# A decoder layer on one core: two of its norms read features-first inputs

## The chip, the cores and the metric

The kernel runs on one core of a Trainium2 chip. The core has a tensor engine (PE, with its weight loads listed as PEld), a vector engine (DVE), a scalar engine (ACT), GpSimd (POOL) and SyncE (SP), which here only issues transfers. Each engine has its own queue of instructions and takes them in order; semaphores hold an instruction until its inputs are there. DMA engines move data between main memory and the on-chip memory of 128 partitions; transfers are issued from the queues of SP, ACT and POOL. Matmuls write to eight PSUM banks of 128 x 512 fp32.

The metric is the device time of one execution in microseconds (us), and the median over several runs.

## What is computed

One layer of a decoder for 256 tokens of 2048 features, in fp32. Cut to what matters here:

```python
def rms_norm(x, g):
    y = x * rsqrt(mean(x * x, axis=-1) + 1e-6)
    return y * g

def swiglu(h, w_gate, w_up, w_down):
    return (silu(h @ w_gate) * (h @ w_up)) @ w_down

x = x + 0.5 * swiglu(rms_norm(x, ffn1_norm), ffn1_w_gate, ffn1_w_up, ffn1_w_down)
x = gated_parallel_mixer(x, mix_norm, w_in, ...)   # attention beside RWKV-7, then w_out
h, mn = rms_norm(x, cross_norm), rms_norm(mem, mem_norm)
x = x + attend(h @ w_cross_q, mn @ w_cross_kv) @ w_cross_o
x = x + 0.5 * swiglu(rms_norm(x, ffn2_norm), ffn2_w_gate, ffn2_w_up, ffn2_w_down)
return rms_norm(x, final_norm)
```

`x` and `mem` are both 256 x 2048. The feed-forward width is 5632. Five norms feed products; the change concerns the two that read inputs of the kernel, that of `x` in front of the first feed-forward and that of `mem`.

## The kernel before

**Products.** PE contracts over partitions, so the activations of a product must lie features first: 16 chunks of 128 features, each a tile of 128 features x 256 tokens. To keep fp32 accuracy each operand is split in a high half (rounded to the matmul's type) and a low half, the difference; `times` (line 426) issues three matmuls per chunk: high by high (L429), high by low (L430), low by high (L431). A `multiply` does two chunks for one half of the tokens, that is six matmuls; an *item* is two chunks of one block of 512 weight columns, so it has two multiplies, twelve matmuls. A product over 2048 features has eight items.

**Weights.** SP loads raw weights into buffers (`load`, tag raw2 with three buffers, two items each, in the feed-forward), ACT casts them to the high half (L341), DVE subtracts to the low half (L342). `next_item` loads ahead and splits up to two items ahead of the one in use; high and low halves have three buffers each.

**The order of work.** `Interleave` holds side jobs as generators in groups (const, feat, attn, ew, chain, norm, mem, in this order). Every multiply is followed by one `tick`, in which each group steps its first jobs once. `product` ticks until the chunks of an item are there (`x.done`), then issues the item. Issue order on the engines follows this, except that an instruction may be put ahead of an earlier one that has to wait; `tc.issue_after` forbids this against one given instruction.

**The norms.** A `Norm` scales by the gain while the data are moved and applies the factor 1/rms later, at the product's result, since it is one number per token. `block` handles 512 features: for two chunks at a time `feat` (L626) makes four PE transposes of 128 x 128 into a PSUM bank, ACT writes the high half times the gain (L653), DVE the low half (L654). Then two ACT squares with a sum along the row (L662) give the sums of squares per token. After the fourth block `rstd` adds the four sums (L672), scales (L673) and lets POOL raise them to the power -1/2 (L675). The first reader of the factor is the Silu of the first product (L710), which empties a PSUM bank; the tag `acc` has three banks and a product takes two.

**The start.** PE first runs nine matmuls on a tile of ones (L185). The gains and other vectors come as rows of 128 and are transposed on PE (`row_vectors`): the first gain at once (L249, L250), 64 gain columns and 83 other columns about 20 ticks later (`late_vectors`). SP loads the first 512 columns of x (L764), the first weights (one piece on ACT's queue), the second block of x (L766) and so on in turn. x stays in place and takes the residual sums of the feed-forward.

**mem.** During the w_out products a job loads each of the four mem blocks by POOL's queue into a tile of tag t4 (20 buffers) and normalises it like x. The same tag holds the x2 tiles, into which POOL loads the stored x (L1369).

Of the kernel before, what the change touches and what calls it, by code (L numbers as in the profile page):

```python
# [139 lines left out]
def decoder_layer(ctx: ExitStack, tc: tile.TileContext, a: dict, out: bass.AP):  # L140
# [27 lines left out]
    def tr():  # L168
        return ps.tile([P, 512], F32, tag="tr", name="tr", bufs=2)
# [11 lines left out]
    pool.memset(ones[:], 1.0)  # L181

    idle_bank = mm()
    for _ in range(9):
        pe.matmul(idle_bank[:, :P], ones[:], ones[:], start=True, stop=True)  # L185

    def select(out, in_, pattern, op, fill, base, mult):
# [40 lines left out]
    pool.dma_start(sinks[:], a["attn_sinks"].broadcast_to([P, 16]))  # L228


    def row_vectors(rows, name, queue):

        n = len(rows)
        r = cpool.tile([n, P], F32, name=name + "_r")
        at = 0
        while at < n:
            src, lo = rows[at]
            m = 1
            while at + m < n and rows[at + m][0] is src and rows[at + m][1] == lo + m * P:
                m += 1  # L240
            queue.dma_start(
                r[at : at + m, :], src[lo : lo + m * P].rearrange("(c p) -> c p", p=P)
            )
            at += m
        v = cpool.tile([P, n], F32, name=name)

        def fill():
            t = tr()
            pe.transpose(t[:, :n], r[:], ident[:n, :n])  # L249
            return act.copy(v[:], t[:, :n])  # L250

        return v, fill

    def flat(x):
        x = x[0]
        return x if len(x.shape) == 1 else x.rearrange("h d -> (h d)")

    def chunks(names, n):
        return [(v, c * P) for v in (flat(a[m]) for m in names) for c in range(n)]

    g_ffn1, fill = row_vectors(chunks(["ffn1_norm"], KD), "g_ffn1", act)
    first = fill()
    rows = chunks(["mix_norm", "cross_norm", "mem_norm", "ffn2_norm"], KD)
    gains, fill_gains = row_vectors(rows, "gains", pool)
    g_mix, g_cross, g_mem, g_ffn2 = (gains[:, i * KD : (i + 1) * KD] for i in range(4))
    per_head = ("w0", "a0", "k_k", "k_a", "r_k", "ln_w", "ln_b")
    rows = chunks(["rwkv_" + n for n in per_head], 8)
    v = flat(a["rwkv_mu"])
    rows += [(v, c * P) for c in range(26)] + [(v, 3360 - P)]
    rv, fill_rv = row_vectors(rows, "rv", pool)  # L270
    w0, a0, k_k, k_a, r_k, ln_w, ln_b = (rv[:, i * 8 : (i + 1) * 8] for i in range(7))
    mu = rv[:, 56:83]
    nk_k = cpool.tile([P, 8], F32, name="nk_k")
# [1 line left out]

    def late_vectors():
        yield from idle(20)
        fill_gains()
        fill_rv()
        dve.tensor_scalar(nk_k[:], k_k, -1.0, None, ALU.mult)  # L280
        dve.tensor_scalar(ok_a[:], k_a, -1.0, 1.0, ALU.mult, ALU.add)

# [66 lines left out]

    WHOLE = ((slice(0, KU), nullcontext),)  # L350
    ONE = ((slice(0, 1), nullcontext),)

    def sums(raw):

# [14 lines left out]
    def divide(i):  # L369
        if i >= len(items) or i in parts:  # L370
            return
        raw = raws[i]
        if not paired(i):
            each = [(slice(j, j + 1), lambda: tc.issue_after(first.ins)) for j in range(KU)]
            parts[i] = split_raw(raw, each if i < AHEAD else WHOLE)
        elif items[i][4]:
            t = sums(raw)
            u1, g1 = split_raw(raw[:, 2:4], WHOLE)
            g0, _ = split_raw(raw[:, 0:2], ONE)
            parts[i] = (g0, g1, u1), t  # L380
# [255 lines left out]
    class Norm:  # L636
# [9 lines left out]
        def block(self, n, src):  # L646
# [18 lines left out]
            if n == 3:  # L665
                yield
                self.r = rstd(self.ss[:])

    def rstd(ss):
        n = ss.shape[1]  # L670
        m = stat.tile([P, n], F32, tag="ms", name="ms")
        dve.tensor_reduce(m[:], ss, AX.X, ALU.add)  # L672
        dve.tensor_scalar(m[:], m[:], 1.0 / D, EPS, ALU.mult, ALU.add)  # L673
        r = stat.tile([P, n], F32, tag="rs", name="rs")
        pool.tensor_tensor(r[:], m[:], nhalf[:, :n], ALU.pow)  # L675
        return [r[:, t : t + 1] for t in range(n)]


    def feed_forward(sp, x, norm: Norm, wg, wu, wd, done, begin_last=lambda: None, last=False):
        if last:  # L680
            for tag, shape, dt, bufs in (
                ("hhi", [P, 16, T], F32R, 1), ("hlo", [P, 16, T], F32R, 1),
                ("hb", [P, 2, 512], F32, 2), ("thi", [P, 4, 512], F32R, 1),
                ("tlo", [P, 4, 512], F32R, 1),
            ):
                sp.tile(shape, dt, tag=tag, name=tag, bufs=bufs)
        c = combinations(sp, norm.x, SEVEN, EARLY, lambda: norm.r is not None, "c", 4)
        for gi, (j0, nj) in enumerate(GROUPS):
            h = Act(
                [sp.tile([P, 16, T], F32R, tag="hhi", name="hhi")],  # L690
                [sp.tile([P, 16, T], F32R, tag="hlo", name="hlo")], 16,
            )

            def transposed(hb, c):
                for q in range(2):
                    split(h, c + 2 * q, 2, feat(hb, [2 * q * P, (2 * q + 1) * P]))
                    yield

            for j in range(j0, j0 + nj):
                if j > 0:  # L700
                    hb = gate_up(sp, norm.x, c, norm.r, wg)

                    c["next"].append(transposed(hb, 4 * (j - j0)))
                    if j == j0 + nj - 1:
                        bg.spawn("feat", c["next"].pop())
                    continue
                pg = product(norm.x, wg)
                hb = sp.tile([P, 2, 512], F32, tag="hb", name="hb", bufs=2)
                for t in range(2):
                    act.activation(hb[:, t, :], pg[t][:], AF.Silu, scale=norm.r[t])  # L710
                pu = product(norm.x, wu)
                for t in range(2):
                    dve.scalar_tensor_tensor(
                        hb[:, t, :], pu[t][:], norm.r[t], hb[:, t, :], ALU.mult, ALU.mult
                    )
                bg.spawn("feat", transposed(hb, 4 * (j - j0)))
            end = gi == len(GROUPS) - 1
            if end:
                begin_last()
            d = combinations(sp, h, SEVEN_DOWN, (), lambda: True, "d", 0)  # L720
            for n in (0, 2):
                if n in down_pairs(gi):
                    down(
                        sp, h, d, wd,
                        lambda t, m, w, n=n: x[:, t, (n + m) * 512 : (n + m + w) * 512],
                        [lambda m=m: done(m) for m in (n, n + 1)] if end else [],
                    )
                    continue
                for m in (n, n + 1):
                    pd = product(  # L730
                        h, wd, skew=last and end and m == 3, bank=mm if m == 2 else acc
                    )
                    for t in range(2):
                        xs = x[:, t, m * 512 : (m + 1) * 512]
# [7 lines left out]
    W = {n: v[0] for n, v in a.items()}  # L742
# [12 lines left out]
    with tc.tile_pool(name="f1", bufs=1, reuse_waits="tile") as sp:  # L755
# [4 lines left out]
        def col(n):  # L760
            return x[:, :, n * 512 : (n + 1) * 512]

        n1 = Norm(g_ffn1)
        nc.sync.dma_start(col(0), blk(W["x"], 0))  # L764
        load(0, ((slice(0, 1), act), (slice(1, 2), nc.sync), (slice(2, 4), nc.sync)))
        nc.sync.dma_start(col(1), blk(W["x"], 1))  # L766
        load(2, ((slice(0, 2), nc.sync), (slice(2, 4), nc.sync)))
        for n in range(2, 4):
            nc.sync.dma_start(col(n), blk(W["x"], n))
            load(2 * n)  # L770
        for n in range(4):
            bg.spawn("feat", n1.block(n, col(n)))
        bg.spawn("const", late_vectors())
        hold = {}

        def done1(n):
# [11 lines left out]
    with tc.tile_pool(name="mx", bufs=1, reuse_waits="tile") as sp:  # L788
# [568 lines left out]

        def memory():
            for n in range(4):
                s = t4("mem", (P, 2, 512))  # L1360
                pool.dma_start(s[:], blk(W["mem"], n))
                yield from idle(3)
                yield from nm_.block(n, s)

        x2 = []
        for n in range(4):
# [133 lines left out]
                queue.dma_start(out[0, t * P : (t + 1) * P, cb], x[:, t, cb])  # L1500


_INS = [
    "x", "mem", "ffn1_norm", "ffn1_w_gate", "ffn1_w_up", "ffn1_w_down", "mix_norm", "w_in",
    "attn_sinks", "rwkv_mu", "rwkv_w0", "rwkv_w2", "rwkv_a0", "rwkv_a2", "rwkv_g2", "rwkv_k_k",
# [27 lines left out]
```

## Time and profile before

| | us |
|---|---|
| three runs | 2270.74, 2272.89, 2273.24 |
| median | 2272.89 |
| profiled execution, its own time | 2270.65 |
| its span, first to last instruction | 2268.9 |
| mean granted PE clock in it | 0.998 |

The profile is one execution. Busy times are per engine, and an engine's idle time is put down to what came last before it went on ("releaser"). A row of a timeline gives start and duration in us, engine, line, operation, written tile <- read tiles, and the count where equal neighbours are merged. Rows by stretch give the stretch, its length, then busy time and instructions of PE, PEld, DVE, ACT and POOL (or of PE alone), then the granted clock of PE as a share of full speed, the busy share of the DMA engines and GB/s. Chain rows give the start and length of each piece of the chain of work that ended last. A group row gives busy us and the mean ns of one instruction, then the idle time ahead of it. Matmul ends are modelled, so the distance between starts is what one takes. An fp32 matmul shows as two records.

### The profile page before, as it was taken

The numbers are of one execution on the slowest core, as the hardware profiler recorded it, in microseconds if no ns is written. First come the engines' busy times: TensorE is split into PE (matmuls) and PEld (weight loads), VectorE is DVE, ScalarE is ACT, GpSimd is POOL, SyncE is SP. The second block draws the span as 40 slices with busy tenths as digits, with TensorE's granted clock in tenths as the row PEclk, the third lists the DMA queues.
The fourth block names the chain that finished last, engine by engine and source line by source line (L and its number), as shares of the span: only waits on it lengthen the run. The fifth ranks groups of instructions, "written<-read, shape, count | busy, mean of one in ns | idle before, by whom it ended". The sixth has DMA issues, their size and how long they took to land.

```text
span 2268.9 us, 28433 instructions
## 1 busy us (share of the span) xinstructions
PE 2252.7 (99%) x10635; PEld 1847.8 (81%) x10635; DVE 1735.9 (77%) x2114; ACT 1214.1 (54%) x1638; POOL 131.4 (6%) x191
## 2 busy tenths in 40 slices
PE   9999999999999999999999999999999999999998
PEld 7888888888888778788888888888888888888886
DVE  6988988888987567795444556547888888898987
ACT  6555555555555576444344446456555455555554
POOL 2000000000000002101220030001000000000002
PEclk9999999999999999999999999999999999999999
DMA  7666665566666545776433576657655666566664
GB/s 242 198 204 190 196 214 188 185 211 199 202 200 199 143 140 161 217 222 199 118 99 89 167 261 222 204 164 253 204 187 190 206 200 202 191 199 204 197 204 156
DMA packets 222922, 432.53 MB, mean 191 GB/s; under 512 B 17883, under 2 KB 20160, under 8 KB 222784
## 3 DMA queue, kind: packets, MB, share of 16 engines
q1 hardware_dynamic: 214208, 404.80, 55.7%
q0 software_dynamic: 8112, 25.12, 3.5%
q8 instruction: 83, 1.36, 0.3%
q10 hardware_dynamic: 464, 0.79, 0.1%
q14 instruction: 55, 0.45, 0.1%
HBM read 417.56 MB, written 13.11 MB: 190 GB/s over the span
## 4 chain that ended last, share of the span: by engine, by line
PE 96%; DVE 2%; issue 1%; ACT 1%; DMA 0%; POOLq 0%; POOL 0%; ACTq 0%; SPq 0%; DVEq 0%
PE acc L429 20%; PE acc L430 20%; PE acc L431 20%; PE mm L431 8%; PE mm L429 8%; PE mm L430 8%; PE tr L626 2%; PE tr L430 2%; PE tr L431 2%; PE tr L429 2%; PE mm L1230 1%; PE tr L1199 1%; DVE lo L342 0%; PE mm L829 0%; ACT hi L341 0%
## 5 line engine op out<-in xcount | busy, mean ns | idle before, releaser
L341 ACT CAST hi<-raw 128x1024 fp32r<-128x1024 f32 (+1 forms) x770 | 763.6, 1000 | 781.6 <-PE acc L431 389.4
L342 DVE TENSOR_TENSOR lo<-raw,hi 128x1024 fp32r<-128x1024 f32 (+1 forms) x770 | 892.4, 1169 | 375.3 <-ACT hi L341 374.2
L429 PE MATMUL acc<-hi,xhi 128*128 128x512 f32 (+1 forms) x1196 | 478.0, 400 | 1.4 <-ACT xhi L653 1.4
L430 PE MATMUL acc<-lo,xhi 128*128 128x512 f32 (+1 forms) x1196 | 466.2, 390 | 1.9 <-DVE lo L342 1.9
L431 PE MATMUL acc<-hi,xlo 128*128 128x512 f32 (+1 forms) x1196 | 465.1, 389 | 0.0
L429 PEld LDWEIGHTS acc<-hi,xhi 128*128 128x128 f32 x1196 | 225.2, 188 | 50.7 <-issue 5.4
L430 PEld LDWEIGHTS acc<-lo,xhi 128*128 128x128 f32 x1196 | 225.5, 189 | 47.0 <-issue 2.7
L431 PEld LDWEIGHTS acc<-hi,xlo 128*128 128x128 f32 x1196 | 224.9, 188 | 47.8 <-DVE xlo L654 0.9
L365 ACT CAST thi<-raw 128x1024 fp32r<-128x1024 f32 x160 | 165.9, 1051 | 77.4 <-DVE raw L362 38.6
L366 DVE TENSOR_TENSOR tlo<-raw,thi 128x1024 fp32r<-128x1024 f32 x160 | 193.3, 1222 | 1.7 <-ACT thi L365 1.7
L430 PE MATMUL acc<-lo,hhi 128*128 128x512 f32 x404 | 158.1, 391 | 0.0
L431 PE MATMUL acc<-hi,hlo 128*128 128x512 f32 x404 | 158.0, 391 | 0.0
L429 PE MATMUL acc<-hi,hhi 128*128 128x512 f32 x404 | 157.4, 392 | 0.0
L429 PE MATMUL mm<-hi,xhi 128*128 128x512 f32 x380 | 149.3, 393 | 0.0
L431 PE MATMUL mm<-hi,xlo 128*128 128x512 f32 x380 | 148.3, 390 | 0.0
L430 PE MATMUL mm<-lo,xhi 128*128 128x512 f32 x380 | 148.2, 390 | 0.0
L360 DVE TENSOR_TENSOR raw<-raw 128x1024 f32<-128x1024 f32 x80 | 98.0, 1225 | 25.2 <-DMA raw<-in_ffn_w_up_dram 23.3
L430 PEld LDWEIGHTS acc<-lo,hhi 128*128 128x128 f32 x404 | 75.9, 188 | 17.4 <-DVE lo L342 2.3
L429 PEld LDWEIGHTS acc<-hi,hhi 128*128 128x128 f32 x404 | 75.9, 188 | 15.9 <-DVE x L584 0.9
L431 PEld LDWEIGHTS acc<-hi,hlo 128*128 128x128 f32 x404 | 75.9, 188 | 15.4
L430 PEld LDWEIGHTS mm<-lo,xhi 128*128 128x128 f32 x380 | 71.4, 188 | 15.2 <-DVE lo L342 0.2
L431 PEld LDWEIGHTS mm<-hi,xlo 128*128 128x128 f32 x380 | 71.3, 188 | 14.7
(385 smaller groups left out, 3428.4 us busy)
## 6 DMA issues: line engine op xcount, KB each, us to landing
raw<-in_ffn_w_gate_dram SPq DMA_DIRECT2D x167, 512.0 KB, 3.8
raw<-in_ffn_w_up_dram SPq DMA_DIRECT2D x160, 512.0 KB, 4.7
raw<-in_ffn_w_down_dram SPq DMA_DIRECT2D x152, 512.0 KB, 4.7
raw<-in_w_in_dram SPq DMA_DIRECT2D x136, 512.0 KB, 3.7
raw<-in_w_out_dram SPq DMA_DIRECT2D x32, 512.0 KB, 4.6
raw<-in_ffn_w_down_dram SPq DMA_DIRECT2D x12, 1024.0 KB, 5.2
raw<-in_ffn_w_up_dram SPq DMA_DIRECT2D x8, 1024.0 KB, 5.9
raw<-in_w_proj_attn_dram SPq DMA_DIRECT2D x16, 512.0 KB, 3.6
```

The lines of the kernel that those rows point to most:

```text
L341: newest["act"] = act.copy(hi[:, s], raw[:, s])
L342: newest["dve"] = dve.tensor_tensor(lo[:, s], raw[:, s], f32(hi[:, s]), ALU.subtract)
L360: dve.tensor_tensor(ta[:], raw[:, 1:3], raw[:, 0:2], ALU.subtract)
L365: act.copy(hi[:, s], t[:])
L366: dve.tensor_tensor(lo[:, s], t[:], f32(hi[:, s]), ALU.subtract)
L429: pe.matmul(o, xh, hi, start=first, stop=False, **how)
L430: pe.matmul(o, xh, lo, start=False, stop=False, **how)
L431: pe.matmul(o, xl, hi, start=False, stop=last, **how)
L626: pe.transpose(b[:, o : o + P], tok[:, t, col : col + P], ident[:])
L1199: pe.matmul(b[e][:, m * P : (m + 1) * P], x1[r, j, cs_], x2[r, j, cs_], start=True, stop=True,)
L1230: pe.matmul(vb[:, o : o + P][:, r], lhs(e), rhs[:, r], start=first and e == 0, stop=True, **ek,)
```

## The change

On the host, x and mem are also laid out as `xT` and `memT` with 128 partitions x 16 chunks x 256 tokens, and the vectors as columns: `g_first` (128 x 16), `g_later` (128 x 64), `v_rwkv` (128 x 83). The rows of x are still an input.

- `row_vectors`, its transposes and copies go; `vectors` loads each array with one transfer (g_first on ACT's queue, the others on POOL's, where 13 loads were).
- 11 matmuls on ones instead of 9.
- The x norm and the mem norm use `features` and `squares` instead of `block`: no transposes; ACT and DVE read the loaded tile; ACT then squares that tile in place, DVE adds the four squared tiles into the first, adds its two pairs of chunks, and PE contracts the result with a column of ones, two matmuls for each half of the tokens. `rstd` then starts at the scaling.
- x comes in the order 2 chunks, weights, 2 chunks, weights, 4 chunks, weights and so on, into tiles that the feed-forward uses later (tags hb and thi); a fifth weight load is issued up front. The rows of x for the residual are loaded by POOL about 24 ticks apart.
- The first two items are split in single chunks without the order against the first gain.

```diff
-    for _ in range(9):
+    for _ in range(11):
         pe.matmul(idle_bank[:, :P], ones[:], ones[:], start=True, stop=True)
...
+    def vectors(name, n, queue):
         v = cpool.tile([P, n], F32, name=name)
+        queue.dma_start(v[:], a[name])
+        return v
...
+    g_ffn1 = vectors("g_first", KD, act)
+    gains = vectors("g_later", 4 * KD, pool)
+    rv = vectors("v_rwkv", 83, pool)
...
         yield from idle(20)
-        fill_gains()
-        fill_rv()
...
+    EACH = tuple((slice(j, j + 1), nullcontext) for j in range(KU))
...
-            each = [(slice(j, j + 1), lambda: tc.issue_after(first.ins)) for j in range(KU)]
-            parts[i] = split_raw(raw, each if i < AHEAD else WHOLE)
+            parts[i] = split_raw(raw, EACH if i < AHEAD else WHOLE)
...
+        def features(self, n, src, total):
+            for j in range(4):
+                c = 4 * n + j
+                g = self.gain[:, c : c + 1]
+                last = act.activation(self.x.at(0, c), src[:, j, :], AF.Copy, scale=g)
+                dve.scalar_tensor_tensor(
+                    self.x.at(1, c), src[:, j, :], g, f32(self.x.at(0, c)),
+                    ALU.mult, ALU.subtract,
+                )
+                self.x.done.add(c)
+                if j % 2:
+                    self.last = last
+                    yield
+            bg.spawn("ew", self.squares(n, src, total))
+
+        def squares(self, n, src, total):
+            with tc.issue_after(self.last.ins):
+                act.activation(src, src, AF.Square)
+            yield
+            if n:
+                dve.tensor_tensor(total, total, src, ALU.add)
+            if n < 3:
+                return
+            yield
+            dve.tensor_tensor(total[:, :2], total[:, :2], total[:, 2:], ALU.add)
+            yield
+            b = tr()
+            for t in range(2):
+                for k in range(2):
+                    pe.matmul(
+                        b[:, t : t + 1], total[:, k, t * P : (t + 1) * P], ones[:, :1],
+                        start=t + k == 0, stop=t + k == 2, skip_group_check=True,
+                    )
+            self.r = rstd(b[:, :2].unsqueeze(2))
...
                 pg = product(norm.x, wg)
+                bg.until(lambda: norm.r is not None)
...
-        nc.sync.dma_start(col(0), blk(W["x"], 0))
+        turned = [sp.tile([P, 4, T], F32, tag="hb", name="xt", bufs=2) for _ in range(2)]
+        pair = sp.tile([P, 8, T], F32, tag="thi", name="xt")
+        turned = [v[:] for v in turned] + [pair[:, :4], pair[:, 4:]]
+        nc.sync.dma_start(turned[0][:, :2], a["xT"][:, 0:2])
         load(0, ((slice(0, 1), act), (slice(1, 2), nc.sync), (slice(2, 4), nc.sync)))
-        nc.sync.dma_start(col(1), blk(W["x"], 1))
+        nc.sync.dma_start(turned[0][:, 2:], a["xT"][:, 2:4])
         load(2, ((slice(0, 2), nc.sync), (slice(2, 4), nc.sync)))
-        for n in range(2, 4):
-            nc.sync.dma_start(col(n), blk(W["x"], n))
-            load(2 * n)
+        for n in range(1, 4):
+            nc.sync.dma_start(turned[n], a["xT"][:, 4 * n : 4 * n + 4])
+            load(2 * n + 2)
         for n in range(4):
-            bg.spawn("feat", n1.block(n, col(n)))
+            bg.spawn("feat", n1.features(n, turned[n], turned[0]))
...
+        def residual():
+            for n in range(4):
+                yield from idle(24)
+                pool.dma_start(col(n), blk(W["x"], n))
+
+        bg.spawn("chain", residual())
...
         def memory():
             for n in range(4):
-                s = t4("mem", (P, 2, 512))
-                pool.dma_start(s[:], blk(W["mem"], n))
+                s = t4("mem")
+                pool.dma_start(s[:], a["memT"][:, 4 * n : 4 * n + 4])
+                if n == 0:
+                    total = s
                 yield from idle(3)
-                yield from nm_.block(n, s)
+                yield from nm_.features(n, s[:], total[:])
```

More of the change, by code (lines that the diff above doesn't have):

```diff
@@ L228, in decoder_layer @@
     pool.dma_start(sinks[:], a["attn_sinks"].broadcast_to([P, 16]))
[L231 to L244, printed above, removed]
-        v = cpool.tile([P, n], F32, name=name)
[L247 to L264, printed above, removed]
-    g_mix, g_cross, g_mem, g_ffn2 = (gains[:, i * KD : (i + 1) * KD] for i in range(4))
[L266 to L270, printed above, removed]
+    def vectors(name, n, queue):
+        v = cpool.tile([P, n], F32, name=name)
+        queue.dma_start(v[:], a[name])
+        return v
+    g_ffn1 = vectors("g_first", KD, act)
+    gains = vectors("g_later", 4 * KD, pool)
+    g_mix, g_cross, g_mem, g_ffn2 = (gains[:, i * KD : (i + 1) * KD] for i in range(4))
+    rv = vectors("v_rwkv", 83, pool)
     w0, a0, k_k, k_a, r_k, ln_w, ln_b = (rv[:, i * 8 : (i + 1) * 8] for i in range(7))
@@ L671, in rstd @@
         m = stat.tile([P, n], F32, tag="ms", name="ms")
-        dve.tensor_reduce(m[:], ss, AX.X, ALU.add)
-        dve.tensor_scalar(m[:], m[:], 1.0 / D, EPS, ALU.mult, ALU.add)
+        if ss.shape[2] > 1:
+            dve.tensor_reduce(m[:], ss, AX.X, ALU.add)
+            ss = m[:].unsqueeze(2)
+        dve.tensor_scalar(m[:], ss[:, :, 0], 1.0 / D, EPS, ALU.mult, ALU.add)
         r = stat.tile([P, n], F32, tag="rs", name="rs")
@@ L740, in blk @@
         return d[:, n * 512 : (n + 1) * 512].rearrange("(t p) n -> p t n", p=P)
-    W = {n: v[0] for n, v in a.items()}
+    W = {n: v[0] for n, v in a.items() if n not in _LAID}
     x1d = dram.tile([T, D], F32, name="x1d")
@@ L1500, in decoder_layer @@
                 queue.dma_start(out[0, t * P : (t + 1) * P, cb], x[:, t, cb])
+_LAID = ("xT", "memT", "g_first", "g_later", "v_rwkv")
 _INS = [
@@ L1520, with turned, columns @@
     )
+    laid = {n: _np.asarray(inputs[n]) for n in _INS}
+    def turned(v):
+        return v[0].reshape(T, KD, P).transpose(2, 1, 0)
+    def columns(names):
+        return _np.concatenate([laid[n].reshape(-1, P) for n in names]).T
+    mu = laid["rwkv_mu"].reshape(-1)
+    per_head = ("w0", "a0", "k_k", "k_a", "r_k", "ln_w", "ln_b")
+    laid["xT"], laid["memT"] = turned(laid["x"]), turned(laid["mem"])
+    laid["g_first"] = columns(["ffn1_norm"])
+    laid["g_later"] = columns(["mix_norm", "cross_norm", "mem_norm", "ffn2_norm"])
+    laid["v_rwkv"] = _np.concatenate([
+        columns(["rwkv_" + n for n in per_head]),
+        mu[: 26 * P].reshape(26, P).T, mu[-P:].reshape(P, 1),
+    ], axis=1)
     arrays, args = {}, {}
-    for name in _INS:
-        v = _np.ascontiguousarray(inputs[name])
+    for name in laid:
+        v = _np.ascontiguousarray(laid[name])
         arrays[f"in_{name}_dram"] = v
```

## The prediction

> **What bounds the kernel now.** I read the page first, then the busy time by stretch, then the list of what the tensor engine (PE) waited for.
>
> ```profile
> span 2268.9 us, 28433 instructions
> PE 2252.7 (99%) x10635; PEld 1847.8 (81%) x10635; DVE 1735.9 (77%) x2114; ACT 1214.1 (54%) x1638; POOL 131.4 (6%) x191
> PE 96%; DVE 2%; issue 1%; ACT 1%; DMA 0%; POOLq 0%; POOL 0%; ACTq 0%; SPq 0%; DVEq 0%
> ...
> 20.00:40.00 20.00, 20.00 (x94) 16.34 (x93) 13.97 (x23) 16.83 (x31) 0.73 (x1) 1.00 0.62 205
> 40.00:60.00 20.00, 20.00 (x92) 16.08 (x90) 18.24 (x29) 11.25 (x15) 0.00 (x0) 1.00 0.55 177
> 60.00:80.00 20.00, 20.00 (x90) 16.31 (x89) 19.48 (x26) 11.59 (x14) 0.00 (x0) 1.00 0.58 194
> ...
> 1400.00:1420.00 20.00, 20.00 (x101) 16.27 (x100) 14.28 (x23) 15.86 (x33) 1.44 (x2) 1.00 0.47 155
> ...
> PE acc L430 <- DVE lo L342: 1.9, 1, 1.9
> PE acc L429 <- ACT xhi L653: 1.4, 1, 1.4
> ```
>
> PE is busy 99% of the span and carries 96% of the chain that ended last. The rows by stretch give busy time of PE, PE's weight loads, DVE, ACT and POOL, then the granted clock: between 20 and 80 us, and where mem is normalised (1400 to 1420), PE has no hole. So an instruction taken from PE's queue there is worth its whole issue time, and one taken from ACT or DVE nothing, until they become late. DVE is close to that at 60 to 80 (19.48 of 20). The only long waits in the list are one for the first copy of x (1.4) and one for a weight half (1.9).
>
> **The start.** The timeline's rows give start, duration and instruction. The rows from 1.29 on are two of the chain (start, length) and the first two x loads, which end in the us from issue to landing.
>
> ```profile
> 0.81 0.44 SPq L764 DMA_DIRECT2D x<-in_x_dram  x1
> 1.06 4.21 PE L185 MATMUL mm<-ones 128*128 128x128 f32 x18 [1.06 <-POOL ones L181]
> 2.28 0.47 SPq L766 DMA_DIRECT2D x<-in_x_dram  x1
> 5.36 1.09 PE L626 MATMUL tr<-ident,x 128*128 128x128 f32 x8
> 6.82 0.62 ACT L341 CAST hi<-raw 128x512 fp32r<-128x512 f32 x1 [1.18 <-DMA raw<-in_ffn_w_gate_dram]
> 7.35 0.47 ACT L653 ACTIVATE xhi<-tr,g_ffn 128x256 fp32r<-128x256 f32 x1
> 7.87 0.50 PE L429 MATMUL acc<-hi,xhi 128*128 128x512 f32 x1 [1.42 <-ACT xhi L653]
> ...
> 34.79 0.39 PE L431 MATMUL acc<-hi,xlo 128*128 128x512 f32 x1
> ...
> 1.29 5.51 DMA raw<-in_ffn_w_gate_dram
> 16.30 0.44 PE tr L626 x4
> ...
> x<-in_x_dram SPq DMA_DIRECT2D x1, 512.0 KB, 4.4
> ...
> x<-in_x_dram SPq DMA_DIRECT2D x1, 512.0 KB, 7.3
> ```
>
> The first real matmul (7.87) stands behind the first weight piece (landed 1.29 + 5.51 = 6.80), its cast, and then the scaled copy of x, which ACT does only after that cast. x's first block landed at 0.81 + 4.4 = 5.2 with 512 KB ordered ahead of and with it, its second at 2.28 + 7.3 = 9.6 with 2048 KB: 1536 KB in 4.4 us, or 2.9 us per MB in the order of issue. By that the first weight piece, inside the first 1024 KB, should land at 6.7; it landed at 6.80, so the rule of thumb holds.
>
> After the change the first x piece is 256 KB, so this weight piece is inside the first 768 KB: 5.2 + 0.25 x 2.9 = 5.9 to 6.0. x itself lands near 4.5, its copy needs no transpose, and is done before; PE starts at 6.0 + 0.62 + 0.04 = 6.65 instead of 7.87: **1.2 us gained** (bounds: 0, if the column load of g_first in front of it on ACT's queue holds it, to 1.4).
>
> The product that follows issues 96 matmuls, from 7.87 to 35.02 (34.79 and one issue of 0.23): 27.15 us. At 0.23 a matmul they take 22.0. Eight transposes were done before the start; the other 24 are six groups of four at 0.44 on the chain: **2.65 us gained** exactly where PE has no hole. The rest, 27.15 - 22.0 - 2.65 = 2.5, is clock and waits.
>
> ```profile
> 8.00:9.00 1.00, 1.00 (x4) 0.66 (x5) 1.00 (x3) 1.00 (x3) 0.81 (x2) 0.78 1.10 393
> 9.00:10.00 1.00, 1.00 (x4) 0.81 (x3) 1.00 (x3) 0.72 (x2) 0.00 (x0) 0.50 0.95 290
> ...
> 11.00:12.00 1.00, 1.00 (x4) 0.71 (x4) 0.00 (x0) 0.71 (x1) 0.85 (x2) 0.52 1.06 393
> 12.00:13.00 1.00, 1.00 (x7) 0.78 (x6) 0.63 (x1) 0.93 (x3) 0.81 (x3) 1.00 1.06 396
> ...
> 960.00:964.00 4.00, 2.14 (x10) 1.69 (x10) 3.83 (x11) 0.72 (x1) 0.00 (x0) 1.00 0.36 96
> ```
>
> The third number from the end is the granted clock: it is halved for about 3.4 us (22% of the stretch from 8 to 9 is 0.44 short, then 0.5 each), which costs 1.7 us of PE's work. PE had stood 1.42 us before it. Yet at 960 to 964 it stood 1.86 of 4 us and the clock stayed at 1.00, so idle time alone doesn't settle it. In the new kernel 11 warm-up matmuls make 22 records of 4.21 / 18 = 0.234 us, to 1.06 + 5.15 = 6.2; the hole up to 6.65 is 0.45 us instead of 1.42, so I take the clock as kept. [...]
>
> Against it, the 2.5 us are not all won. x's order in the queue is worse: the third piece now stands behind items 2 and 3 of the weights, with 3072 KB before and in it, so it lands at 5.2 + 2.5 x 2.9 = 12.5; item 2 wants it at 6.65 + 2 x 2.75 + 0.7 (the first low half, 0.69 on DVE behind its cast) = 12.9, and a copy of 0.47 stands between. I allow 1.3 us of waits (0.7 and 0.6; bounds 0 and 2.5, the latter all that there was): **1.2 us gained** from the 2.5.
>
> **The sums.** One square of 128x1024 per block on ACT replaces two of 128x512 with read-outs; DVE gets three adds of 128x1024 and one of 128x512; PE gets four matmuls with one column per norm; scale, power and Silu follow as before.
>
> ```profile
> L342 DVE TENSOR_TENSOR lo<-raw,hi 128x1024 fp32r<-128x1024 f32 x16 | 19.6, 1224 | 9.5 <-ACT hi L341 9.5
> L461 DVE TENSOR_TENSOR u<-xhi,xlo 128x512 f32<-128x512 f32 x4 | 2.7, 686 | 0.0
> L341 ACT CAST hi<-raw 128x1024 fp32r<-128x1024 f32 x10 | 10.5, 1050 | 3.4 <-DMA raw<-in_ffn_w_gate_dram 1.6 <-PE acc L431 1.4 <-PE tr L626 0.4
> ...
> 1100.99 0.56 PE L1230 MATMUL mm<-u,xb 128*128 128x64 f32 x4
> 1101.38 0.61 PE L1213 MATMUL tr<-vtok,mk 128*128 128x64 f32 x4
> ...
> 32.01 0.48 DVE L654 SCALAR_TENSOR_TENSOR xlo<-tr,g_ffn,xhi 128x256 fp32r<-128x256 f32 x1
> 33.12 0.73 POOL L675 TENSOR_TENSOR rs<-ms,nhalf 128x2 f32<-128x2 f32 x1 [19.24 <-DVE ms L673]
> 33.90 1.28 ACT L710 ACT_TABLE_LOAD   x1 [0.35 <-PE acc L431]
> 35.20 1.27 ACT L710 ACTIVATE hb<-acc,rs 128x512 f32<-128x512 f32 x2
> ```
>
> An fp32 matmul is two records (9 made 18 above); four small ones take 1101.38 - 1100.99 = 0.39, so eight take **0.8 us lost** per norm (bounds 0.4 and, at the warm-up's 0.234 a record, 1.9). DVE's extra is 3 x 1.22 + 0.69 = 4.35 us, in a stretch where it is busy 13.97 of 20: covered there, and a delay if moved to 60 to 80.
>
> The wait is the delicate part. The norm's factor was ready at 33.12 + 0.73 = 33.85, before the product's end; Silu then freed the first bank. The next product starts on a third bank, 6 matmuls of 0.23 or 1.36 us, and then needs that bank. In the new code the last block's sums are spread over ticks 12 to 15 of 16, a tick being six matmuls, where they were at 12 and 13; the four matmuls stand in PE's in-order queue in front of the last item, and everything behind them waits if the sum is late. The last x piece stands on SP behind the fourth weight load, which waits until items 0 and 1 are split, and should land near 5.2 + 5.5 x 2.9 = 21.2 (6144 KB); copies, square and adds with weight work between end at 27 to 29, PE is there at about 27.2. I take **0.4 us lost** (bounds 0 and 3.9, the rival below).
>
> **The rest.**
>
> ```profile
> 40.62 0.43 PE tr L249 x2
> ...
> L626 PE MATMUL tr<-ident,mem x32: 270/272/303, 1386.2 to 1413.4; 128*128 128x128 f32 x32
> ...
> 1393.20 0.72 POOL L1369 DMA_DIRECT2D x<-x1d  x1 [25.59 <-ACT junk L662]
> 1428.92 1.28 DVE L1372 TENSOR_TENSOR x<-acc,x 128x512 f32<-128x512 f32 x2
> ...
> 217.78 2.36 DVE L603 TENSOR_TENSOR x<-hb,x 128x1024 f32<-128x1024 f32 x2
> ```
>
> The two transposes of the vectors go: **0.43 gained**. The mem norm drops 32 transposes, 8 groups of 0.44 = **3.5 gained**, and pays **0.8 lost**; its adds lie under DVE's 14.28 and ACT's 15.86 of 20, and its factor isn't wanted until the w_out products are over. POOL's third load of x1d waited for a mem tile (1393.20). If that tile is now the running sum, it comes free after mem's last matmuls, some four ticks behind 1413.4, about 1419; its reader is at 1428.92, and a 512 KB load took 7.3 in the crowded start: hidden, by 2 to 3 us. POOL loses 11 of its 13 small vector loads, which held nobody. x for the residual now comes by POOL in four loads of 0.72 us issue and 512 KB, about 25 ticks (34 us) apart, first read at 217.78 and covered; beside 0.55 to 0.62 DMA share they cost nothing, uncovered up to 1.4 us each.
>
> **The sum**: 1.2 + 2.65 + 1.2 - 0.8 - 0.4 + 0.43 + 3.5 - 0.8 = **7.0 us**. The profiled execution took 2270.65 (span 2268.9 and 1.75 around it): 2263.7 by its own time. The three runs shown are 2270.74, 2272.89 and 2273.24; from their median, 2265.9. I forecast **2266**.
>
> **Rivals.**
>
> *The clock falls again, or x comes later than worked out.* The clock fell once for reasons the rows don't separate, and the DMA order is worse for x. It takes back up to the 1.7, and 0.5 more waits: gain 4.8, **2268**.
>
> *The factor is late.* If ACT and DVE reach the last block no earlier than now (32.01 + 0.48 = 32.5, 2.5 us before the product's end), then square 1.05, add 1.22, add 0.69, matmuls 0.8, scale 0.2 (estimate), power 0.73, table 1.28, Silu 0.64 and some 1.2 of handovers (estimate, eight at 0.15) end 5.3 us after the product's end; PE can bridge 1.36. It stands 3.9 instead of 0.4: gain 3.5, **2269.4**. For it: the present order does put x's last copies that late. Against: they then waited for transposes, which are gone.
>
> *Slower: DVE becomes the bound of the first feed-forward stage.* It is full from about 47 to 80 us. If its work and not PE's sets when the first pass ends, all gain of the front is lost, its 4.35 us come on top, and the combinations, which start on the factor, begin two ticks (2.7 us) later: 4.35 + 2.7 - (0.43 + 2.7) = 3.9 slower, **2276.8**. It decides from the point where PE waits for a low half after 47 us. Against: PE has no such wait there now, and DVE idles 6 us between 20 and 40, room for the adds.
>
> **Chances.** Forecast 0.54, clock or x 0.20, late factor 0.15, DVE 0.11. The 0.2% (4.5 us) is about what a measurement of this kernel can tell from no change: below 2268.4 is faster. Nearly all of the forecast, half of the clock's case and a quarter of the late factor's are there: 0.51 + 0.10 + 0.04 = 0.65. The rest of these, with a little of DVE's, is the same: 0.24; slower, DVE above all, 0.11. The range: best case all 2.5 us won, start 1.4, sums at 0.4 each without wait, 1.4 + 2.65 + 2.5 + 3.93 - 0.8 = 9.7, with 1 us of spread 2262; on the other side the late factor with the spread of the runs and part of DVE's case, 2272.
>
> **What would show it.** First real matmul at 6.6 to 6.8; clock 1.00 through 8 to 12; product's last matmul near 30.5; no PE wait on the one-column matmuls or on Silu above 0.5; no transposes between 1386 and 1413. A half clock, a wait on the sums, or waits for low halves at 50 to 80 us would each point to its rival; an unchanged start with x's pieces awaited would prove the transfer sum wrong.

## The result and the profile after

The changed kernel takes 2275.16 us (median of 22 runs, 2273.36 to 2279.44); the kernel before, run beside it, 2272.34 (22 runs). The ratio is 1.0015 with a 95% interval of 1.0008 to 1.0021: some 3 us slower, where 7 us faster were forecast. The profiled execution has a span of 2273.3, against 2268.9.

The page of the changed kernel, and its list of what PE waited for (total us, times, longest):

```profile
span 2273.3 us, 28304 instructions
PE 2248.3 (99%) x10588; PEld 1842.6 (81%) x10588; DVE 1742.7 (77%) x2120; ACT 1213.6 (53%) x1611; POOL 128.9 (6%) x184
PE 93%; DVE 3%; DMA 2%; issue 1%; ACT 1%; POOL 0%; SPq 0%; POOLq 0%; ACTq 0%; DVEq 0%
```

```profile
PE acc L396 <- ACT xhi L642: 4.6, 2, 2.5
PE tr L397 <- DVE tlo L334: 2.1, 2, 1.7
PE acc L397 <- DVE lo L309: 2.0, 2, 1.8
PE acc L396 <- ACT hi L308: 1.7, 1, 1.7
PE acc L396 <- ACT hb L717: 1.4, 1, 1.4
...
PE tr L593 <- DVE x L1391: 1.0, 2, 0.7
```

PE has 47 records and 4.4 us less work, and yet the span is 4.4 us longer: PE stands idle 8.8 us more (25.0 for 16.2). The chain shows DMA (2%, 0 before), and the list names the scaled copies of x (L642 is the old L653). The timeline of the changed kernel says when and why:

```profile
6.48 2.85 POOL L788 DMA_DIRECT2D x<-in_x_dram  x4
6.83 0.73 PE L396 MATMUL acc<-hi,xhi 128*128 128x512 f32 x2 [1.66 <-ACT hi L308]
14.75 1.71 ACT L642 ACTIVATE xhi<-xt,g_first 128x256 fp32r<-128x256 f32 x4 [1.38 <-DMA xt<-in_xT_dram]
15.31 0.50 PE L396 MATMUL acc<-hi,xhi 128*128 128x512 f32 x1 [2.47 <-ACT xhi L642]
21.52 1.04 ACT L308 CAST hi<-raw 128x1024 fp32r<-128x1024 f32 x1 [3.45 <-DMA raw<-in_ffn_w_gate_dram]
23.19 0.50 PE L396 MATMUL acc<-hi,xhi 128*128 128x512 f32 x1 [2.14 <-ACT xhi L642]
36.08 0.39 PE L398 MATMUL acc<-hi,xlo 128*128 128x512 f32 x1
37.21 0.95 PE L667 MATMUL tr<-ones,xt 128*128 128x1 f32 x8
38.28 1.23 DVE L309 TENSOR_TENSOR lo<-raw,hi 128x1024 fp32r<-128x1024 f32 x1
38.52 1.57 POOL L681 TENSOR_TENSOR rs<-ms,nhalf 128x2 f32<-128x2 f32 x1 [29.18 <-DVE ms L679]
40.87 0.50 PE L396 MATMUL acc<-hi,xhi 128*128 128x512 f32 x1 [1.43 <-ACT hb L717]
```

The first real matmul is at 6.83, a good microsecond earlier than before, as forecast. But the first row is decisive: POOL issues **all four loads of x's rows at once**, from 6.48 to 9.33, and not 25 ticks apart. They are 2 MB more in the stretch in which every weight and every piece of x is awaited. The transfers of the first 40 us (count, size, median us from issue to landing), then the stretches (busy time of PE, PEld, DVE, ACT and POOL, granted clock, DMA share, GB/s):

```profile
raw<-in_ffn_w_gate_dram SPq DMA_DIRECT2D x2, 1024.0 KB, 16.4
x<-in_x_dram POOLq DMA_DIRECT2D x4, 512.0 KB, 10.5
...
xt<-in_xT_dram SPq DMA_DIRECT2D x3, 512.0 KB, 16.5
```

```profile
12.00:16.00 4.00, 1.53 (x7) 0.98 (x6) 2.17 (x5) 2.29 (x5) 0.00 (x0) 1.00 1.03 398
16.00:20.00 4.00, 4.00 (x20) 3.27 (x19) 2.36 (x6) 1.52 (x3) 0.00 (x0) 1.00 1.03 387
20.00:24.00 4.00, 1.68 (x7) 0.86 (x6) 1.40 (x2) 2.42 (x4) 0.00 (x0) 1.00 1.03 391
24.00:28.00 4.00, 4.00 (x11) 3.12 (x12) 4.00 (x7) 3.75 (x7) 0.00 (x0) 0.57 1.04 394
...
60.00:80.00 20.00, 20.00 (x90) 16.10 (x90) 20.00 (x29) 12.09 (x14) 0.00 (x0) 1.00 0.57 189
```

```profile
20.00:24.00 4.00, 4.00 (x21) 3.21 (x19) 2.43 (x4) 4.00 (x9) 0.00 (x0) 1.00 0.63 232
24.00:28.00 4.00, 4.00 (x23) 3.20 (x22) 2.90 (x6) 3.67 (x10) 0.00 (x0) 1.00 0.78 236
```

The last two rows are the kernel before. There the crowd had thinned by 20 us (DMA share 0.63); in the changed kernel it is full to 28 us. The 1 MB weight loads took 16.4 us each where before's took 10.7. PE has two holes, 2.47 and 2.14, and behind the second one its clock falls to half for 3.4 us (0.57 in the row 24 to 28), 1.7 us of work. The first product's 96th matmul starts at 36.08, 1.29 later than before instead of 4 to 5 earlier.

### The profile page after: what moved, and what is told of

Read it like the earlier page. It is cut to its first block, busy times and chain, and to the rows that moved or that the text cites. A ratio compares the mean times of both kernels' runs of the same rounds, so it can differ in the third digit from the quotient of the medians.

```text
span 2273.3 us, 28304 instructions
## 1 busy us (share of the span) xinstructions
PE 2248.3 (99%) x10588; PEld 1842.6 (81%) x10588; DVE 1742.7 (77%) x2120; ACT 1213.6 (53%) x1611; POOL 128.9 (6%) x184
## 4 chain that ended last, share of the span: by engine, by line
PE 93%; DVE 3%; DMA 2%; issue 1%; ACT 1%; POOL 0%; SPq 0%; POOLq 0%; ACTq 0%; DVEq 0%
PE acc L396 19%; PE acc L397 19%; PE acc L398 19%; PE mm L397 8%; PE mm L398 8%; PE mm L396 8%; PE tr L593 2%; PE tr L397 2%; PE tr L398 1%; PE tr L396 1%; PE mm L1247 1%; DVE lo L309 1%; PE tr L1216 1%; DMA raw<-in_ffn_w_gate_dram 1%; DMA raw<-in_ffn_w_up_dram 1%
```

## The experiments

All are timed against the kernel before on the same chip. For the profiles, this table gives how much later (+) or earlier (-) than in the profile of before a kernel is: at the 96th and the 192nd matmul of the first feed-forward (the ends of its first two products), at the first store of x1d (691.24 before), at the first read of km (1502.4 before, behind mem's stage), and in the span.

| | 96th | 192nd | x1d | km | span | ratio of times, 95% |
|---|---|---|---|---|---|---|
| after | +1.29 | +3.43 | +5.0 | +3.5 | +4.4 | 1.0015 (1.0008 to 1.0021) |
| e1 rows held | -4.30 | -2.05 | -0.8 | +0.2 | -0.9 | 0.9989 (0.998 to 0.9998) |
| e2 no rows | -4.77 | -2.54 | -0.5 | -2.6 | -3.2 | 0.9988 (0.9979 to 0.9997) |
| e3 before + loads | +6.37 | +6.38 | +7.0 | +8.5 | +7.7 | 1.0024 (1.0015 to 1.0033) |
| e4 mem as before | +1.50 | +5.24 | +6.7 | +9.2 | +8.2 | 1.0022 (1.0013 to 1.0031) |
| e5 x as before | +4.81 | +4.30 | +6.0 | +3.8 | +3.4 | 1.0008 (1.0 to 1.0017) |
| e6 held, mem as before | -4.51 | -2.27 | -1.3 | -1.4 | -0.7 | 0.9996 (0.9987 to 1.0004) |
| e7 held, first pow | -4.72 | -0.89 | 0.0 | -0.1 | +0.4 | 0.9982 (0.9973 to 0.999) |
| e8 e7, x2 later | -4.04 | -1.79 | -1.5 | -3.5 | -3.2 | 0.9979 (0.997 to 0.9988) |
| e9 pow before low half | -4.64 | -3.30 | -1.6 | -1.8 | -0.6 | 0.9981 (0.9973 to 0.999) |
| e10 e9, x piece earlier | -3.15 | -1.95 | -1.2 | -1.3 | +1.1 | 0.9989 (0.998 to 0.9998) |
| e11 before + mem part | +0.11 | +0.11 | +1.8 | -0.4 | -1.1 | 0.9989 (0.998 to 0.9998) |

A row is one execution, and equal code can differ in it. e4 has the code of the changed kernel up to mem, yet its 192nd matmul is 1.8 later: its clock fell once more, from 41.2 to 44.6. e11 has the code of before up to mem, yet it loses 1.7 between the 192nd matmul and x1d, 0.96 of it in one wait for a low half. A single difference of that size settles nothing.

**Are the rows the cause?** Three kernels: hold them, leave them out, or give the kernel before the same four loads.

e1 records the newest weight load of SP (`newest["sp"]`) and issues the rows on SP behind it:

```diff
             for n in range(4):
                 yield from idle(24)
-                pool.dma_start(col(n), blk(W["x"], n))
+                with tc.issue_after(newest["sp"].ins):
+                    nc.sync.dma_start(col(n), blk(W["x"], n))
```

> The four loads of x's rows are issued by SP in between the paired weight loads from 45 us on, instead of by POOL at 6.5 us. Theory (the rows crowd the first weights and x pieces): the third x piece lands near 12.5 instead of 14.7, the third pair of weights near 15.5 instead of 21.5, the first product's last matmul is issued near 31 instead of 36.1, the clock stays at 1.00, and the time falls by 4 to 6 us against the changed kernel, to 2269 to 2271. Rival (the pieces of x come too late by their own order): last matmul still at 34 or later, time 2273 or more. A third part, the one-column matmuls and the wait for Silu (2.4 us together in the changed kernel), should stay under either.

e2 fills the rows with zeros; x is left out of the residual sum of the first feed-forward:

```diff
-                pool.dma_start(col(n), blk(W["x"], n))
+                pool.memset(col(n), 0.0)
```

> The rows of x aren't loaded at all; POOL fills the residual tile with zeros at the start, so that x is left out of the residual sum. Theory: same as with the rows held back, within 0.7 us, since loads spread over the first stage cost nothing. Rival (2 MB more traffic costs wherever it stands): 2 us or more faster than with the rows held back.

e3 adds to the kernel before four loads that nobody reads:

```diff
     pool.dma_start(sinks[:], a["attn_sinks"].broadcast_to([P, 16]))
+    for n in range(4):
+        extra = wp.tile([P, KU, 512], F32, tag="raw", name="extra", bufs=4)
+        pool.dma_start(extra[:], a["mem"][0][:, n * 512 : (n + 1) * 512].rearrange(...))
```

> The kernel before, with four extra loads of 512 KB by POOL from 5.4 us on, into buffers that nothing reads. Theory (2 MB more in the first 25 us delay weights and x): the first product ends 3 to 5 us later than at 35.0 and the time is 2275 to 2277.5. Rival (only the changed order of x's pieces makes the loads harmful): under 1 us slower, 2272 to 2273.5.

e1 takes 2269.57, e2 2268.12, e3 2276.07, with 2271.26 for the kernel before. Held or absent, the rows cost the same within the intervals, and the same loads make the kernel before slower by 0.24%. There the first product ends 6.37 later, more than the 3 to 5 expected: behind waits of 2.98 and 1.25 the clock stood at half from 13.7 to 23.9. From after to e1 the 192nd matmul moves by 3.43 + 2.05 = 5.5 us, 1.7 of it the changed kernel's fall of the clock. e1's timeline:

```profile
6.94 0.73 PE L398 MATMUL acc<-hi,xhi 128*128 128x512 f32 x2 [1.74 <-ACT hi L310]
14.12 0.50 PE L398 MATMUL acc<-hi,xhi 128*128 128x512 f32 x1 [1.16 <-ACT xhi L644]
30.49 0.39 PE L400 MATMUL acc<-hi,xlo 128*128 128x512 f32 x1
...
31.63 1.05 PE L669 MATMUL tr<-ones,xt 128*128 128x1 f32 x8
...
35.38 0.50 PE L398 MATMUL acc<-hi,xhi 128*128 128x512 f32 x1 [1.46 <-ACT hb L719]
```

So the early loads of the rows are the cause of the loss. e1 changes both their time and their queue; no run issues them late on POOL's queue or early on SP's, so what the queue adds was not separated. But even without them only 1.7 (e1) to 3.1 us (e2) of the 7 come out by the medians, 2.5 and 2.7 by the ratios. Where do the others go?

**mem's part.** e4 gives the changed kernel the old mem job, e6 does the same with the rows held:

```diff
-                s = t4("mem")
-                pool.dma_start(s[:], a["memT"][:, 4 * n : 4 * n + 4])
...
-                yield from nm_.features(n, s[:], total[:])
+                s = t4("mem", (P, 2, 512))
+                pool.dma_start(s[:], blk(W["mem"], n))
+                yield from idle(3)
+                yield from nm_.block(n, s)
```

> The changed kernel with mem loaded as rows and normalised with transposes, as before the change. Theory (mem's part wins 3.5 us of transposes, pays 0.95 for the one-column matmuls and 1.2 us of waits behind mem's copies on DVE): 1 to 1.7 us slower than the changed kernel, 2276 to 2277. Rival (the waits would be there anyway): 2.5 us slower. Rival (mem's part costs more than it wins): faster than the changed kernel.

> Rows held as in e1 (SP, behind the latest weight load), and mem by rows with transposes as before: x's part alone, freed of the crowd of loads. Theory: x's gain of 4.3 at the end of the first product is given back by 0.95 for the one-column matmuls and 1.46 for the late factor, so 2.05 are left at the 192nd matmul and 1 to 1.5 at 690 us; time 1 to 1.5 under before, 0 to 2 over e1. Rival (mem's part is worth its full 2.7 and x's part nothing): equal to before, 1.7 over e1.

e5 puts x's part of the changed kernel back (rows on SP, `block`, 9 warm-up matmuls). e11 goes from the other side: the kernel before with `memT`, `features`, `squares` and the new `rstd` for mem alone.

> The changed kernel with x's part undone: x comes as rows, on SP, with transposes, read-outs and 9 warm-up matmuls as before; mem comes features first with the sums over features, and the vectors as columns. Theory (mem's transposes sat where PE had no hole, so 3.5 us go and 0.95 come for the one-column matmuls; PE then meets the residual add of x2 on DVE without that cover and waits 0.4 to 1.2): 0.43 + 3.5 - 0.95 - 0.8 = 2.2 us faster than before, 2269.1 (2268.5 to 2270); the first product's 96th matmul at 34.8 as before; a PE wait on x2's residual add of 0.4 to 1.8 where before has none. Rival (the whole of mem's gain is given back behind its copies on DVE): within 0.7 of before.

> The kernel before with mem's part of the change alone (mem features first, squares and sums over features); x, the vectors and the start are as before, unlike in e5, where the casts of the first weight pieces had moved ahead of the first scaled copy of x. Theory: 3.5 for mem's transposes, less 0.95 for the one-column matmuls and 0.3 to 1 for the residual add of x2: 1.5 to 2.3 under before, unless the clock falls behind that wait, as in e1. The first product ends as before (96th matmul at 34.8). Rival (e1: mem's part is worth nothing at all): within 0.5 of before.

e4 takes 2276.2 (before 2271.26), e6 2271.37 and e5 2275.12 (before 2272.44), e11 2269.47 (before 2272.13). mem's part is thus worth 0.07% between e4 and the changed kernel, 0.07% between e6 and e1, and 0.11% in e11: 1.6 to 2.5 us, of the 2.7 forecast. The intervals of the first two pairs overlap, and e11's just stays below 1, so the times alone do not settle it. The trace does: in the table the step from x1d to km is -0.1 in e6, with mem as before, and -2.2 in e11, -2.2 in e5, -2.1 in e2 and -2.0 in e8. In e7, e9 and e10 it is -0.1 to -0.2, with a fall of the clock, worth 1.7, near 960 us in each. In the changed kernel it is -1.5, and in e1 +1.0. e1's timeline and stretches show why:

```profile
1381.21 1.28 DVE L1394 TENSOR_TENSOR x<-acc,x 128x512 f32<-128x512 f32 x2
1381.95 0.33 PE L595 MATMUL tr<-ident,x 128*128 128x128 f32 x1 [1.55 <-DVE x L1394]
```

```profile
1380.00:1384.00 4.00, 2.18 (x9) 1.40 (x8) 4.00 (x6) 3.81 (x7) 0.08 (x1) 0.88 0.69 224
1384.00:1388.00 4.00, 4.00 (x16) 3.20 (x16) 3.23 (x6) 1.94 (x4) 0.64 (x1) 0.69 0.66 200
```

PE wants to transpose x2 while the residual add still stands on DVE. In before and e6 mem's own transposes lay between, and there is no such wait; in e11, which differs from before in mem alone, there is one of 0.3. The removed work was also a cover, if not always a full one: e4 has mem's transposes and waits twice for 0.3. In e1 the clock fell too behind the wait of 1.55 (0.88, 0.69), and mem's gain was gone.

e5's total misses its expectation by 6 us, and for a reason of its own. With x as rows, the dropped order against the first gain lets ACT cast all four weight pieces (7.56 and 8.92) ahead of the first copy of x:

```profile
7.56 1.14 ACT L308 CAST hi<-raw 128x512 fp32r<-128x512 f32 x2 [4.47 <-DMA raw<-in_ffn_w_gate_dram]
8.92 1.14 ACT L308 CAST hi<-raw 128x512 fp32r<-128x512 f32 x2 [0.22 <-DMA raw<-in_ffn_w_gate_dram]
9.96 0.47 ACT L620 ACTIVATE xhi<-tr,g_first 128x256 fp32r<-128x256 f32 x1
```

PE waits 3.23 for it, and the clock stands at half from 8.0 to 18.2. "x as before" was not x as before; e11 was run for that.

**The late factor.** e1, e2, e7 and e8 all wait 1.4 to 1.46 for Silu. The pow took 1.57 where 0.73 was forecast. e7 puts an idle pow at the start:

```diff
     pool.memset(nhalf[:], -0.5)
+    first_pow = cpool.tile([P, 2], F32, name="first_pow")
+    pool.tensor_tensor(first_pow[:], ones[:, :2], nhalf[:], ALU.pow)
```

> e1 with one more pow on POOL, of ones, at 6.5 us right behind the memsets, its result read by nobody. Theory A (POOL's pow for the first norm took 1.57 where the later ones take 0.73 because it is the first): the factor's pow takes 0.73, Silu starts 0.85 earlier, PE's wait for it falls from 1.46 to 0.6, and the time is 0.85 under e1. Theory B (the 1.57 comes from where the pow stands, after 26 us without work on POOL): it takes 1.57 again and the time is e1's.

e8 also lets the work on each x2 block start a tick later:

```diff
-            bg.spawn("feat", n3.block(n, s))
+            def later(n=n, s=s):
+                yield
+                yield from n3.block(n, s)
+
+            bg.spawn("feat", later())
```

> e7, and the work that turns each block of x2 (PE's transposes of it, its copies and sums) begins one tick, six matmuls or 1.36 us, later behind the residual add. Theory: PE's wait on that add in mem's stage (0.4 to 1.8 in the runs so far) goes to zero, as the add of two times 0.64 us is covered by one tick, and the time is 0.4 to 1.8 under e7. Rival (DVE is late with its whole queue there, not with the add alone): the wait moves to the next low half or to the copies of x2, and the time is e7's within 0.5.

e7 takes 2268.42, e8 2267.49 (before 2272.44). The idle pow took 0.73 and the factor's pow 1.63 all the same: theory A falls. That e7 is nevertheless below e1 has no cause in its profile; its ratio's interval overlaps e1's. In e8 PE's wait on the residual add went from 0.5 to 0.3, but e9 and e10, with the same later start, wait 0.8. That the step from x1d to km went from -0.1 to -2.0 is the clock, which of the two fell near 960 us in e7 alone, worth 1.7 (last section). The ratios of e7 and e8 do not differ beyond their intervals, so whether the later start of x2 helps is not settled.

What the slow pows share is DVE's low half, begun just ahead of them. e9 takes e8 without the idle pow and turns that order round:

```diff
         pool.tensor_tensor(r[:], m[:], nhalf[:, :n], ALU.pow)
+        if gate:
+            newest["gate"] = dve.tensor_copy(m[:], r[:])
...
+            g = newest.pop("gate", None)
+            with tc.issue_after(g.ins) if g else nullcontext():
                 newest["dve"] = dve.tensor_tensor(lo[:, s], raw[:, s], f32(hi[:, s]), ALU.subtract)
```

> e8 without the idle first pow, and with the next low half on DVE kept behind the first norm's pow on POOL (a copy of 128x2 on DVE that reads the factor stands ahead of it). In every profile so far in which a low half of 1.22 us began just before this pow, the pow took 1.57 to 1.63 and ended 0.6 behind that low half; where DVE was idle at its start (before, e3, e5, and the idle pow of e7 and e8) it took 0.73. Theory (POOL is held while DVE's low half runs): the pow takes 0.73, Silu starts 0.85 earlier, PE's wait for Silu falls from 1.4 to 0.6, and the low half behind it ends 0.8 later than in e8 without PE waiting for it; time 0.8 under e8, and more in those executions in which the clock fell behind that wait. Rival (the 1.6 belongs to the pow at this place): the pow takes 1.6, DVE is late by as much, and the time is e8's or up to 1.5 over it.

The timeline of e9:

```profile
31.68 0.73 POOL L687 TENSOR_TENSOR rs<-ms,nhalf 128x2 f32<-128x2 f32 x1 [25.09 <-DVE ms L685]
...
32.52 2.35 DVE L313 TENSOR_TENSOR lo<-raw,hi 128x1024 fp32r<-128x1024 f32 x2
...
33.67 0.50 PE L402 MATMUL acc<-hi,xhi 128*128 128x512 f32 x1 [0.62 <-ACT hb L725]
```

The pow takes 0.73, and PE waits 0.62, both as the theory said. The time does not follow: 2268.35 with 2272.13 before, no better than e8. The 3.30 us won at the 192nd matmul are 1.6 at the first x1d store, as good as the 1.5 in e8 that had won only 1.79. In e9 PE waits 0.25 and 0.73 for low halves of weight sums (tlo) between 300 and 600 us, where e8 has none. About half of what is given back there is these two waits; the rest was not located. e11, with before's code there, gives back as much, so it need not be a cost of e9's edit.

e10 brings the first half of the second 512 KB of x ahead of a weight load:

```diff
-        load(2, ((slice(0, 2), nc.sync), (slice(2, 4), nc.sync)))
+        half = lambda: nc.sync.dma_start(turned[1][:, :2], a["xT"][:, 4:6])
+        load(2, ((slice(0, 2), nc.sync), (half, None), (slice(2, 4), nc.sync)))
+        nc.sync.dma_start(turned[1][:, 2:], a["xT"][:, 6:8])
...
```

> e9, and the second 512 KB of x, features first, comes in two loads of 256 KB, the first of them ahead of the second half of weight items 2 and 3 rather than behind it. Theory (PE's wait of 1.0 to 1.3 for the scaled copy of x at item 2 is order in the queue: 768 KB less stand ahead of it, 2.2 us by the 2.9 us per MB of the start): that wait goes, and the time is 1.0 to 1.3 under e9. Rival (item 3's weights, 256 KB later, are awaited instead; or DVE's low half of item 2 is last anyway): within 0.5 of e9.

It takes 2269.87 (before 2272.13): no gain. The wait for the copy fell from 1.3 to 0.4, but 0.5 for a low half and 0.3 for a low copy of x came in its place, and the 192nd matmul is 1.35 later than in e9. (At the 96th, e10 has the one-column matmuls already behind it and e9 still ahead.) What moved ahead in this queue moved something else back.

## Why the prediction was wrong

**The step that failed** is the last of "The rest": "x for the residual now comes by POOL in four loads ... about 25 ticks (34 us) apart, first read at 217.78 and covered; beside 0.55 to 0.62 DMA share they cost nothing". The ticks place an instruction in the order of issue, and an instruction may be put ahead of an earlier one that has to wait, as the account of the kernel before says. The loads wait for nothing and POOL had only a pow to do, waiting for its input. So they all went at 6.48. What I took as a time was a place in a list. The step cost 5.5 us by e1 and the changed kernel at the 192nd matmul, and it made the clock's rival come true too, by holes that the rows dug. The prediction's own price for uncovered loads, 4 x 1.4 = 5.6, is met by luck: it meant transfers alone, and 1.7 of the 5.5 are the clock. No rival named the rows. The rival on the slower side (2276.8) came near the time with another mechanism: DVE is indeed full at 60 to 80 us (20.00), but PE has no hole there.

**Right, by the same steps.** The start: 1.2 forecast, 7.87 - 6.83 = 1.04 measured. The one-column matmuls: 0.8 forecast, 0.95 measured. PE's wait for the third piece of x: 0.7 and 0.6 allowed, 1.16 in e1.

**Right by luck.** The product's last matmul: near 30.5 forecast, 30.49 in e1. But 30.5 is 34.79 - 1.2 - 2.65 - 1.2 + 0.8, with the one-column matmuls ahead of the last item, and in e1 they run at 31.63, behind the 96th matmul. Like for like, 30.49 stands against 29.7. The term at fault is the 1.2 for clock and waits: 4.30 - 0.93 - 2.65 leaves 0.7. The fall of the clock in before had cost next to nothing, by this pair: e11 has before's start without the fall, and its 96th matmul is 0.11 later, as PE there stood waiting instead.

```profile
12.58 0.50 PE L429 MATMUL acc<-hi,xhi 128*128 128x512 f32 x1 [1.20 <-ACT xhi L653]
```

The clock itself was kept, in e1 up to 40 us, but not for the reason given. The hole ahead of the first matmul was to be 0.45, as the warm-up was to last 5.15; its 22 records took 4.14 in e1 and the hole was 1.74, more than the 1.42 behind which before's clock fell.

**Mis-sized, with the rows away.** The factor's wait: 0.4 forecast, 1.43 to 1.46 measured, and 0.62 in e9, where the pow ran ahead of DVE's low half and took 0.73. mem: its 2.7 are 2.1 to 2.2 where PE waits 0.3 to 0.4 on x2's add, and less where it waits longer; I had looked for what mem's work hides behind, not for what hides behind mem's work. Up to the 192nd matmul the sum has 1.2 + 2.65 + 1.2 - 0.8 - 0.4 + 0.43 = 4.3, and e1 shows 2.05, e2 2.54. Between 55 and 690 us I had nothing: e1 gives back 1.25 there, e2 2.0, e8 0.3, e9 1.7; e11 gives back 1.7 with the code of before, so no run shows that the change costs anything there. Start, product, sums and mem together then make, in e8, 3.5 us at km, and 4.95 in the median.

e8, a 0.21% gain (0.12 to 0.3), is faster than both kernels: the change with the rows held, and x2's transposes a tick later.

## What to carry to other kernels

A delay written as steps of a generator orders instructions; it does not time them. Four loads that waited for nothing went out at once here, from 6.48 us on, and in a start with the DMA engines at a share of 1.03 their bytes were paid by whatever was awaited, 2 MB for some 5.5 us. When work is taken from the bounding engine, ask which of its waits that work was covering, besides what it cost itself.

## What the runs showed of the hardware

**Where the waits lay and where the clock fell.** In each profile whose clock fell ahead of the end (before, the changed kernel, e1, e3, e4, e5, e7, e9, e10) it changes on one grid: a stretch at half clock lasts 3.41 us or a whole multiple of it, as the three steps of e3 from 13.7 to 23.9 (but for the last, which the end cuts off), and the time from one change to any other is a whole multiple too. Here are three stretches of before, the third 660 steps long (length, PE's busy time, clock, DMA share, GB/s):

```profile
5.14:8.55 3.41, 2.00 (x12) 1.00 1.04 396
8.55:11.96 3.41, 3.41 (x9) 0.50 1.04 363
11.96:2264.76 2252.80, 2243.20 (x10599) 1.00 0.59 190
```

One wait is the same in every kernel here, PE's wait of 1.84 to 1.86 for a low half near 960 us. Here it is in before, with the two steps of the grid that it lies in, and then in e9:

```profile
961.94 0.50 PE L430 MATMUL acc<-lo,xhi 128*128 128x512 f32 x1 [1.86 <-DVE lo L342]
```

```profile
957.46:960.87 3.41, 2.62 (x12) 1.00 0.46 173
960.87:964.28 3.41, 2.34 (x10) 1.00 0.34 83
```

```profile
960.21 0.50 PE L403 MATMUL acc<-lo,xhi 128*128 128x512 f32 x1 [1.85 <-DVE lo L313]
```

```profile
957.84:961.25 3.41, 1.56 (x8) 1.00 0.35 119
961.25:964.66 3.41, 3.41 (x10) 0.50 0.87 211
```

In before the wait is cut by a step's end, and neither step has more than 1.07 of idle. In e9 it lies whole in one step, and the next step runs at half clock, which costs half of 3.41, 1.7 us. So it goes in the other profiles: in five of the 13 (e3, e4, e7, e9, e10) the wait lay whole in a step, and the clock fell in each. In the other eight the clock did not fall there; in the four of them in which another fall places the grid (before, the changed kernel, e1, e5) the wait was cut, and no step had more than 1.58 of it. The hole of 2.47 in the changed kernel was cut in 1.39 and 1.08, and the clock stayed. What sets where the grid lies in an execution no run shows: a step ends at 960.87 in before and at 961.25 in e9. With nothing different in the kernel, eight runs of e11 took 2267.77 to 2269.49 at a mean clock of 0.999 and three took 2271.43 to 2271.47 at 0.997. So single profiles are compared stage by stage. How much idle in a step is enough was not settled: the clock stayed behind a step with 1.74 of idle, at e1's start, and fell behind one with 1.42, the first step of before shown above, which also held the eight transposes (5.36 to 6.45).

**POOL's pow took longer beside a low half on DVE.** The first norm's pow took 0.73 with DVE idle at its start and 1.57 to 1.63 when a low half of 1.22 had begun up to 0.25 earlier; in e9, with the low half kept behind it, it took 0.73. In the changed kernel the low half ends at 38.28 + 1.23 = 39.51, the pow 0.58 later. How the low half lengthens the pow no run shows.
